# Hybrid decoder trunk on one core: ScalarE's table load at the top, the first chunk of x transposed as a whole, its rounding in pinned turns by K tile, the squares later

## The chip, the cores and the metric

The kernel runs on one core of one Trainium2 chip. The metric is device time in microseconds (us) of one execution, as the median of several. A core has five engines that run side by side, each in the order of its own instruction queue, and wait for each other by semaphores: TensorE (PE in the profile, its weight loads PEld), VectorE (DVE), ScalarE (ACT), GpSimd (POOL) and SyncE (SP, which here only issues transfers).

## The reference

The model has two layers over 256 tokens of width 2048. Each layer multiplies the normalised input by one wide projection, runs differential attention and a short gated convolution on the pieces, projects back, and then does a squared-ReLU MLP:

```python
for l in range(DEPTH):
    h = _rmsnorm(x, attn_norm_g[l])
    proj = h @ w_in[l]
    q, k, v, gate_b, gate_c, conv_in = jnp.split(proj, splits, axis=-1)
    ...
    x = x + jnp.concatenate([attn, conv.astype(attn.dtype)], axis=-1) @ w_out[l]
    hm = _rmsnorm(x, mlp_norm_g[l]) @ w_up[l]
    x = x + jnp.square(jax.nn.relu(hm)) @ w_down[l]
```

What matters for this case is the very first product, the first 512 columns of q in layer 0: `h @ w_in` over K = 2048. Nothing after it differs between the two kernels in work or order.

## The kernel before, in words

**Precision by halves.** Every fp32 matrix product is made of three products of a rounded type (fp32r). Each operand x is split into hi, which is x rounded by a ScalarE copy, and lo = x - hi, made by VectorE. The product is hi·hi + hi·lo + lo·hi (`TERMS`, L39). So each 128x512 block of weights costs one ScalarE instruction (`whi`, L291) and one VectorE instruction (`wlo`, L292) before TensorE can use it, and each block of activations costs a ScalarE `nT` (L255) and a VectorE `nT` (L256).

**The first product.** `linear` (L348 to L365) runs over 16 K tiles of 128 rows; I call them k0 to k15. A K tile takes six matmuls of 128x512: for each of the two token tiles hi·hi, then activation hi with weight lo, then activation lo with weight hi. The activations come from x by chunk: x is held in four chunks of 512 columns, and chunk n gives the K tiles 4n to 4n+3. The weights come in pieces, each of which holds two K tiles: piece p has the K tiles 2p and 2p+1 (`raw`, then `whi` and `wlo`). There are four buffers for `raw` and three each for `whi` and `wlo` (`wpool`, L111), so the rounding of piece p+3 has to wait until TensorE has used piece p up.

**A chunk.** `Norm.chunk` (L417 to L440) transposes a chunk on TensorE: eight 128x128 transposes into two PSUM banks (L425), two K tiles to a bank. Then `split_gained` (L253) rounds them: ScalarE `nT` hi with the norm's gain, VectorE `nT` lo. At the end two ScalarE squares with a running sum (`junk`, L437) collect the row sums that the norm needs; they are used only after all four chunks. The second instruction of ScalarE on a bank waits until VectorE has finished its first one on that bank.

**What sets the order.** TensorE's queue is in the order of the program. Pieces of work are put into it by a background list: `work.tick()` is called after each K tile (L364), and a piece that yields n is taken up again n ticks later. For the other engines a list scheduler picks the order from its own estimate of times; an instruction wrapped in `late` (L119) keeps its place in the program's order. `first_loads` (L1066) starts the chunks 1 to 3 with a delay of 4n-2 ticks, starts chunk 0 at once, ticks once, and then adds five warm-up matmuls of `ones` (L147). Chunk 0 transposes its first two K tiles, yields (L434), and transposes the other two after k0. With these delays the transposes of chunk n stand one K tile ahead of the first use: after k2, k6 and k10.

**The first transfers.** SyncE issues, in this order, the first half of chunk 0 of x, the first K tile of piece 0, the second half of chunk 0, the second K tile of piece 0, piece 1, chunk 1, pieces 2 and 3, chunks 2 and 3, and then piece 4 as soon as piece 0 is rounded. `by_dist`, `lamv` and the like are small setup for the attention, issued by GpSimd; `rps`, `vps` and `lps` are small matmuls of that setup, `rbc` (L470) is a matmul that spreads the norm's row factors, and `diag` is its input.

## Time and profile before

| | us |
|---|---|
| median of three runs | 2176.13 (2175.25 to 2177.49) |
| the profiled execution's own time | 2177.49 |
| span of its instructions in the profile | 2175.4 |
| TensorE busy | 2141.5 (98%) |
| VectorE busy | 1685.5 (77%) |
| ScalarE busy | 1291.3 (59%) |
| first matmul of q starts at | 7.49 |
| first matmul of k, the next product, starts at | 39.93 |

All times inside the profile count from the start of the span. A row of the timeline gives the start, the duration, the engine, the line, the operation, what is written and from what, the number of instructions that the row joins, and in brackets how long the engine was idle before it and which engine's instruction ended that idle time.

### The profile page before, as it was taken

The numbers are of one execution on the slowest core, as the hardware profiler recorded it, in microseconds if no ns is written. First come the engines' busy times: TensorE is split into PE (matmuls) and PEld (weight loads), VectorE is DVE, ScalarE is ACT, GpSimd is POOL, SyncE is SP. The second block draws the span as 40 slices with busy tenths as digits, with TensorE's granted clock in tenths as the row PEclk, the third lists the DMA queues.
The fourth block names the chain that finished last, engine by engine and source line by source line (L and its number), as shares of the span: only waits on it lengthen the run. The fifth ranks groups of instructions, "written<-read, shape, count | busy, mean of one in ns | idle before, by whom it ended". The sixth has DMA issues, their size and how long they took to land.

```text
span 2175.4 us, 29104 instructions
## 1 busy us (share of the span) xinstructions
PE 2141.5 (98%) x10978; PEld 1818.3 (84%) x10978; DVE 1685.5 (77%) x2341; ACT 1291.3 (59%) x1748; POOL 195.2 (9%) x264
## 2 busy tenths in 40 slices
PE   8999999999999999999999999999999999999999
PEld 7878888888888888788878788888888888887887
DVE  5677655698888888888756676556988888888886
ACT  6456545566666666555554564455666666665553
POOL 3021200000000000200101212000000000002001
PEclk9999999999999999999999999999999999999999
DMA  7654766477777777887655457655777777778884
GB/s 254 184 154 155 240 187 184 162 249 225 234 222 222 227 225 219 260 287 261 245 158 179 147 165 240 186 184 180 237 234 223 223 225 225 229 215 274 290 285 140
DMA packets 286012, 469.70 MB, mean 216 GB/s; under 512 B 10579, under 2 KB 191397, under 8 KB 283056
## 3 DMA queue, kind: packets, MB, share of 16 engines
q1 hardware_dynamic: 267552, 412.13, 60.7%
q0 software_dynamic: 18272, 55.70, 7.4%
q8 instruction: 86, 1.41, 0.3%
q14 instruction: 54, 0.44, 0.1%
q10 hardware_dynamic: 48, 0.02, 0.0%
HBM read 437.37 MB, written 30.43 MB: 215 GB/s over the span
## 4 chain that ended last, share of the span: by engine, by line
PE 92%; DVE 2%; DMA 2%; issue 2%; ACT 1%; POOL 1%; ACTq 0%; POOLq 0%; DVEq 0%
PE upc L855 29%; PE pr L903 12%; PE rt L1057 11%; PE o L361 8%; PE rt L903 4%; PE ci L383 4%; PE gc L383 4%; PE gb L383 4%; PE v L361 4%; PE k L361 4%; PE q L361 3%; DMA uraw<-in_w_up_dram 1%; PE upw L855 1%; PE sc L526 1%; PE pr L985 1%
## 5 line engine op out<-in xcount | busy, mean ns | idle before, releaser
L292 DVE TENSOR_TENSOR wlo<-raw,whi 128x1024 fp32r<-128x1024 f32 (+1 forms) x346 | 425.1, 1230 | 250.7 <-ACT whi L291 249.6
L291 ACT ACTIVATE whi<-raw 128x1024 fp32r<-128x1024 f32 (+1 forms) x346 | 363.9, 1054 | 420.7 <-PE o L361 73.6
L855 PE MATMUL upc<-nT,uhi 128*128 128x512 f32 x1920 | 477.6, 391 | 0.0
L718 ACT ACTIVATE uhi<-uraw 128x1024 fp32r<-128x1024 f32 x256 | 271.1, 1060 | 289.7 <-PE upc L855 254.1
L855 PEld LDWEIGHTS upc<-nT,uhi 128*128 128x128 f32 x1920 | 352.8, 188 | 68.2
L719 DVE TENSOR_TENSOR ulo<-uraw,uhi 128x1024 fp32r<-128x1024 f32 x256 | 312.3, 1220 | 115.4 <-ACT uhi L718 113.0
L855 PEld LDWEIGHTS upc<-nT,ulo 128*128 128x128 f32 x1920 | 261.9, 190 | 18.7
L855 PE MATMUL upc<-nT,ulo 128*128 128x256 f32 x1920 | 267.7, 282 | 0.0
L1057 PE MATMUL rt<-whi,g 128*128 128x512 f32 x672 | 211.1, 389 | 0.0
L361 PE MATMUL o<-whi,cat 128*128 128x512 f32 x512 | 159.5, 390 | 0.0
L1057 PEld LDWEIGHTS rt<-whi,g 128*128 128x128 f32 x672 | 126.1, 188 | 26.2
L1057 PE MATMUL rt<-wlo,g 128*128 128x512 f32 x336 | 130.7, 389 | 0.0
L361 PEld LDWEIGHTS o<-whi,cat 128*128 128x128 f32 x512 | 96.1, 188 | 19.7
L882 POOL DMA_DIRECT2D plain<-f x44 | 31.5, 716 | 830.8 <-DVE f L895 808.2
L895 DVE TENSOR_TENSOR f<-h,f 128x1024 fp32r<-128x1024 f32 (+1 forms) x84 | 102.1, 1216 | 0.0
L361 PE MATMUL o<-wlo,cat 128*128 128x512 f32 x256 | 99.7, 389 | 0.0
L740 DVE TENSOR_TENSOR t13l<-t,t13h 128x1024 fp32r<-128x1024 f32 x80 | 97.8, 1223 | 1.8 <-ACT t13h L739 0.5
L740 DVE TENSOR_TENSOR t24l<-t,t24h 128x1024 fp32r<-128x1024 f32 x80 | 97.3, 1216 | 0.4 <-ACT t24h L739 0.3
L903 PE MATMUL pr<-t13h,f 128*128 128x512 f32 x240 | 93.8, 391 | 0.0
L361 PE MATMUL q<-whi,nT 128*128 128x512 f32 x256 | 85.3, 404 | 3.4 <-ACT whi L291 3.4
L894 ACT ACTIVATE f<-h 128x1024 fp32r<-128x1024 f32 (+1 forms) x84 | 86.1, 1024 | 4.2 <-DVE h L892 4.1
L739 ACT ACTIVATE t24h<-t 128x1024 fp32r<-128x1024 f32 x80 | 84.0, 1050 | 4.5 <-PE rt L903 3.0
(365 smaller groups left out, 3879.1 us busy)
## 6 DMA issues: line engine op xcount, KB each, us to landing
uraw<-in_w_up_dram SPq DMA_DIRECT2D x128, 1024.0 KB, 6.5
raw<-in_w_in_dram SPq DMA_DIRECT2D x191, 512.0 KB, 4.0
draw<-in_w_down_dram SPq DMA_DIRECT2D x64, 1024.0 KB, 5.2
raw<-in_w_down_dram SPq DMA_DIRECT2D x64, 1024.0 KB, 6.2
raw<-in_w_out_dram SPq DMA_DIRECT2D x64, 512.0 KB, 3.7
plain<-f POOLq DMA_DIRECT2D x44, 512.0 KB, 6.4
g<-plain POOLq DMA_DIRECT2D x22, 1024.0 KB, 6.4
hid<-h POOLq DMA_DIRECT2D x20, 256.0 KB, 5.9
```

The costliest lines, as they stand in the source:

```text
L291: a = nc.scalar.activation(hi[:, k], raw[:, k], AF.Copy)
L292: d = nc.vector.tensor_sub(lo[:, k], raw[:, k], hi[:, k].bitcast(F32))
L361: nc.tensor.matmul(acc[:, t], a.ap[:, pa, k % KG, t * P:(t + 1) * P], (hi, lo)[pw][:, j], start=(k == 0 and n == 0), stop=(k == nk - 1 and ...
L383: nc.tensor.matmul(acc[:, f, 0] if part else acc[:, f], wt[:, k % 4, fs], a.ap[:, 0, k % KG] if part else a.ap[:, :, k % KG], start=(part ...
L718: nc.scalar.activation(hi, src, AF.Copy)
L719: nc.vector.tensor_sub(lo, src, hi.bitcast(F32))
L740: keep(nc.vector.tensor_sub(lo, src, hi.bitcast(F32)))
L855: nc.tensor.matmul(acc[:, 0] if part else acc, wt[:, k], a.ap[:, 0, k % KG] if part else a.ap[:, :, k % KG], start=(part == 0 and kh == 0 ...
L894: nc.scalar.activation(f[:, 0, :n], h[:, :n], AF.Copy)
L895: nc.vector.tensor_sub(f[:, 1, :n], h[:, :n], f[:, 0, :n].bitcast(F32))
L903: nc.tensor.matmul(prods[n], f[:, pa, a], b[pw], start=(start and m == 0), stop=(stop and m == 2))
L1057: nc.tensor.matmul(prods[p], blocks[b][:, slot, pa, 2 * k + t], w[pw][:, n], start=(i == PLAIN[0] and k == 0 and m == 0), stop=False)
```

## The change

The change touches only what is done before and during the first product.

1. A ScalarE copy of one column of `ones` into `ngains` is put at the top, so that ScalarE's table load, which precedes the first activation, no longer waits for `ngains`.
2. `Norm.begin` replaces `chunk(0, 0)`: all eight transposes of chunk 0 come before the first matmul of q. The five warm-up matmuls behind them and one tick are gone.
3. The activations of chunk 0 and the pieces 0 and 1 are rounded in turns by K tile (`in_turns`): for each of k0 to k3 ScalarE does `nT`, then `whi` of that K tile, and VectorE the two lo parts likewise. All of these are pinned by `late`. Pieces up to the eighth are pinned too when they are rounded (`halves`).
4. The squares of a chunk come later: six ticks after chunk 0's start, four ticks after the other chunks. `factors` waits for all of them.

```diff
+    ngains = const.tile([P, NG], F32, tag="ngains", name="ngains")
+    nc.scalar.activation(ngains[:, :1], ones[:, :1], AF.Copy)
     warm = bank("warm")
...
         def halves(self, raw, c=slice(None)):
-            first = self.cut and i < 2
-            for k in (slice(0, 1), slice(1, None)) if first else (slice(None),):
-                a = nc.scalar.activation(hi[:, k], raw[:, k], AF.Copy)
-                d = nc.vector.tensor_sub(lo[:, k], raw[:, k], hi[:, k].bitcast(F32))
-                if first:
-                    late(a)
-                    late(d)
-            return hi, lo
+            hi, lo = self.pair(raw)
+            a = nc.scalar.activation(hi, raw, AF.Copy)
+            d = nc.vector.tensor_sub(lo, raw, hi.bitcast(F32))
+            if self.cut and self.traced <= 8:
+                late(a)
+                late(d)
+            return hi, lo
...
+        def in_turns(self, n, split):
+            while self.traced < n:
+                self.traced += 1
+                raw = self.early.pop(0)
+                hi, lo = self.made[len(self.made)] = self.pair(raw)
+                for k in range(2):
+                    split(2 * self.traced - 2 + k)
+                    late(nc.scalar.activation(hi[:, k], raw[:, k], AF.Copy))
+                    late(nc.vector.tensor_sub(lo[:, k], raw[:, k], hi[:, k].bitcast(F32)))
...
                 self.tiles[n].ready = 2 * j + 2
-                if j == 0 and n == 0 and (self.which, self.l) == (0, 0):
-                    yield 1
+            if (self.which, self.l) == (0, 0):
+                yield 4
+            self.squares(n)
...
+        def begin(self, weights):
+            a = self.tiles[0].open()
+            tps = []
+            for j in range(2):
+                tps.append(bank(f"tpb{j}"))
+                for i in range(2):
+                    k = 2 * j + i
+                    for t in range(NT):
+                        nc.tensor.transpose(
+                            tps[j][:, i * S + t * P:i * S + (t + 1) * P],
+                            xs[0][:, t, k * P:(k + 1) * P], ident)
+            weights.in_turns(2, lambda k: split_gained(
+                a, k, tps[k // 2][:, k % 2 * S:(k % 2 + 1) * S], norm_gain(0, 0, k), late))
+            self.tiles[0].ready = KG
+            yield 6
+            self.squares(0)
...
-        work.start(norm.chunk(0, 0))
-        work.tick()
-        warm_up(5)
+        work.start(norm.begin(weights))
```

The order of the instructions moves on ScalarE, VectorE, GpSimd and TensorE up to about the middle of the next product, k, and is the same from there to the end; SyncE's order of transfers is the same throughout. Line numbers of the changed kernel differ: L255 becomes L256, L291 becomes L308 (in turns) or L287, L425 becomes L469 (chunk 0) or L439, L437 becomes L455, L361 becomes L374.

The first place is ScalarE at the start of q. Before, behind the table load (`nT_0` is chunk 0, `nT_1` chunk 1, `tpn` and `tpb` are the PSUM banks with the transposes; `whi` of 128x512 is one K tile of piece 0 or 1, of 128x1024 a whole piece):

```order
L255 ACTIVATE nT_0_162<-tpn_0_163,ngains 128x256 x2
L291 ACTIVATE whi<-raw 128x512 x2
L255 ACTIVATE nT_0_162<-tpn_1_191,ngains 128x256 x2
L437 ACTIVATE junk_0_200,ss_131<-x_83 128x512
L437 ACTIVATE junk_1_202,ss_131<-x_83 128x512
L291 ACTIVATE whi<-raw 128x512 x2
L291 ACTIVATE whi<-raw 128x1024 x2
L255 ACTIVATE nT_1_222<-tpn_0_223,ngains 128x256
```

In the changed kernel the same stretch, from the second K tile on, reads:

```order
L256 ACTIVATE nT_0_163<-tpb_164,ngains 128x256
L308 ACTIVATE whi<-raw 128x512
L256 ACTIVATE nT_0_163<-tpb_169,ngains 128x256
L308 ACTIVATE whi<-raw 128x512
L256 ACTIVATE nT_0_163<-tpb_169,ngains 128x256
L308 ACTIVATE whi<-raw 128x512
L256 ACTIVATE nT_1_220<-tpn_0_221,ngains 128x256
L256 ACTIVATE nT_1_220<-tpn_1_230,ngains 128x256
L256 ACTIVATE nT_1_220<-tpn_0_221,ngains 128x256
L256 ACTIVATE nT_1_220<-tpn_1_230,ngains 128x256
L287 ACTIVATE whi<-raw 128x1024 x2
L455 ACTIVATE junk_0_259,ss_132<-x_83 128x512
```

The two squares of chunk 0 have moved behind the pieces 2 and 3, and these two pieces (the `whi` of 128x1024) have moved behind all four `nT` of chunk 1.

The second place is TensorE around the transposes of chunk 1. Before (`q` is the sum in PSUM, `nT_0` and `nT_1` say which chunk a matmul uses):

```order
L425 MATMUL tpn_0_223<-ident,x_84 128x128 x4
L425 MATMUL tpn_1_232<-ident,x_84 128x128 x4
L361 MATMUL q_178<-whi,nT_0_162 128x512
L361 MATMUL q_178<-wlo,nT_0_162 128x512
L361 MATMUL q_178<-whi,nT_0_162 128x512 x2
L361 MATMUL q_178<-wlo,nT_0_162 128x512
L361 MATMUL q_178<-whi,nT_0_162 128x512
L361 MATMUL q_178<-whi,nT_1_222 128x512
```

In the changed kernel, from the last matmuls of k3 on:

```order
L374 MATMUL q_195<-wlo,nT_0_163 128x512
L374 MATMUL q_195<-whi,nT_0_163 128x512
L439 MATMUL tpn_0_221<-ident,x_84 128x128 x4
L439 MATMUL tpn_1_230<-ident,x_84 128x128 x4
L374 MATMUL q_195<-whi,nT_1_220 128x512
L374 MATMUL q_195<-wlo,nT_1_220 128x512
L374 MATMUL q_195<-whi,nT_1_220 128x512 x2
```

The six matmuls of k3 stood between the transposes of chunk 1 and the first matmul that uses them; now nothing stands there. The same holds for the chunks 2 and 3, whose transposes now stand directly ahead of k8 and k12.

The third place is ScalarE ahead of chunk 3. Before, with the semaphores that a row waits for:

```order
L291 ACTIVATE whi<-raw 128x1024 x2
L255 ACTIVATE nT_3_355<-tpn_0_356,ngains 128x256
L255 ACTIVATE nT_3_355<-tpn_1_365,ngains 128x256
L255 ACTIVATE nT_3_355<-tpn_0_356,ngains 128x256
L255 ACTIVATE nT_3_355<-tpn_1_365,ngains 128x256
L437 ACTIVATE junk_0_374,ss_131<-x_86 128x512
L437 ACTIVATE junk_1_376,ss_131<-x_86 128x512
L291 ACTIVATE whi<-raw 128x1024 x3
```

In the changed kernel the three `whi` are the pieces 6, 7 and 8, and the waits on PE are those for a free `whi` buffer:

```order
L287 ACTIVATE whi<-raw 128x1024 [waits DMAHW5_49,Activation_49]
L287 ACTIVATE whi<-raw 128x1024 [waits DMAHW6_49,PE_49,Activation_49]
L287 ACTIVATE whi<-raw 128x1024 [waits DMAHW7_49,PE_49,Activation_49]
L455 ACTIVATE junk_0_353,ss_132<-x_85 128x512 [waits DMAHW1_49]
L455 ACTIVATE junk_1_355,ss_132<-x_85 128x512
L256 ACTIVATE nT_3_357<-tpn_0_358,ngains 128x256 [waits PE_49]
L256 ACTIVATE nT_3_357<-tpn_1_367,ngains 128x256 [waits PE_49]
L256 ACTIVATE nT_3_357<-tpn_0_358,ngains 128x256 [waits DVE_49]
L256 ACTIVATE nT_3_357<-tpn_1_367,ngains 128x256 [waits DVE_49]
```

Piece 8, which only the next product uses and whose buffer is free once k11 is done, now stands ahead of chunk 3, and so do the squares of chunk 2.

More of the change, by code (lines that the diff above doesn't have):

```diff
@@ L161, in trunk @@
     nc.tensor.transpose(gps[:, :NG], ngv, ident[:NG, :NG])
-    ngains = const.tile([P, NG], F32, tag="ngains", name="ngains")
     nc.vector.tensor_copy(ngains, gps[:, :NG])
@@ L283, in halves, with pair @@
         def halves(self, raw, c=slice(None)):
-            i = len(self.made)
-            shape = [P] + list(raw.shape[1:])
-            hi = wpool.tile(shape, F32R, tag="hi", name="whi")
-            lo = wpool.tile(shape, F32R, tag="lo", name="wlo")
-            first = self.cut and i < 2
-            for k in (slice(0, 1), slice(1, None)) if first else (slice(None),):
-                a = nc.scalar.activation(hi[:, k], raw[:, k], AF.Copy)
-                d = nc.vector.tensor_sub(lo[:, k], raw[:, k], hi[:, k].bitcast(F32))
-                if first:
-                    late(a)
-                    late(d)
-            return hi, lo
+            hi, lo = self.pair(raw)
[5 more added lines that the diff above has]
+            return hi, lo
+        def pair(self, raw):
+            shape = [P] + list(raw.shape[1:])
+            return (wpool.tile(shape, F32R, tag="hi", name="whi"),
+                    wpool.tile(shape, F32R, tag="lo", name="wlo"))
+        def in_turns(self, n, split):
[7 more added lines that the diff above has]
+                    late(nc.vector.tensor_sub(lo[:, k], raw[:, k], hi[:, k].bitcast(F32)))
         cut = False
@@ L432, in chunk, with squares @@
                 self.tiles[n].ready = 2 * j + 2
-                if j == 0 and n == 0 and (self.which, self.l) == (0, 0):
-                    yield 1
+            if (self.which, self.l) == (0, 0):
+                yield 4
+            self.squares(n)
+        def squares(self, n):
+            self.squared += 1
             for t in range(NT):
@@ L440, in chunk @@
                     late(sq)
+        def begin(self, weights):
[14 more added lines that the diff above has]
+            self.squares(0)
         def factors(self):
-            while not all(t.ready == KG for t in self.tiles):
+            while self.squared < D // CH or not all(t.ready == KG for t in self.tiles):
                 yield 1
```

9 lines of the change are left out of this document (5 added, 4 removed).

## The prediction

> **What bounds the kernel now.** I read the page first, for the engine that decides, then the windows of the first 50 us.
>
> ```profile
> PE   2141.5 (98%) x10978; PEld 1818.3 (84%) x10978; DVE 1685.5 (77%) x2341; ACT 1291.3 (59%) x1748; POOL 195.2 (9%) x264
> PE 92%; DVE 2%; DMA 2%; issue 2%; ACT 1%; POOL 1%; ACTq 0%; POOLq 0%; DVEq 0%
> ...
> 0.00:10.00 10.00, 7.09 (x36) 5.91 (x37) 2.71 (x8) 3.27 (x5) 6.79 (x18) 1.00 0.76 244
> 10.00:20.00 10.00, 7.84 (x31) 6.00 (x31) 7.19 (x15) 7.45 (x17) 0.62 (x2) 0.83 0.99 339
> 20.00:30.00 10.00, 10.00 (x47) 7.60 (x46) 6.11 (x10) 7.81 (x16) 0.00 (x0) 1.00 0.49 164
> 30.00:40.00 10.00, 9.57 (x48) 7.58 (x46) 6.37 (x16) 5.78 (x11) 4.03 (x5) 1.00 0.80 225
> ...
> 40.28 15.01 PE k L361 x66
> ```
>
> TensorE is busy for 98% of the span and carries 92% of the chain. So an edit counts only by how much earlier or later it lets TensorE reach the next product, k; from there the order is as before. The windows (length, then busy time of PE, PEld, DVE, ACT and POOL, granted clock, DMA share, GB/s) show idle TensorE and a lowered clock only in the first 20 us, apart from 0.43 us before 40. The chain's row gives the price of a matmul: 15.01 us for 66, 0.227 each, 1.36 a K tile.
>
> ```profile
> 1.72 0.43 SPq L135 DMA_DIRECT2D x<-in_x_dram  x1
> 2.19 0.47 SPq L314 DMA_DIRECT2D raw<-in_w_in_dram  x1
> 2.69 0.43 SPq L316 DMA_DIRECT2D raw<-in_w_in_dram  x1
> x<-in_x_dram SPq DMA_DIRECT2D x1, 256.0 KB, 4.8
> raw<-in_w_in_dram SPq DMA_DIRECT2D x1, 256.0 KB, 5.1
> raw<-in_w_in_dram SPq DMA_DIRECT2D x1, 512.0 KB, 6.2
> 4.01 0.92 PE L425 MATMUL tpn<-ident,x 128*128 128x128 f32 x4 [0.20 <-DMA x<-in_x_dram]
> 4.13 1.28 ACT L255 ACT_TABLE_LOAD   x1 [4.13 <-DVE ngains L163]
> 5.42 0.47 ACT L255 ACTIVATE nT<-tpn,ngains 128x256 fp32r<-128x256 f32 x1
> 7.49 0.50 PE L361 MATMUL q<-whi,nT 128*128 128x512 f32 x1 [1.45 <-ACT whi L291]
> 11.54 0.62 ACT L437 ACTIVATE junk<-x 128x512 f32<-128x512 f32 x1
> 12.77 3.03 ACT L291 ACTIVATE whi<-raw 128x512 fp32r<-128x512 f32 x4
> 13.44 0.50 PE L361 MATMUL q<-whi,nT 128*128 128x512 f32 x1 [1.93 <-ACT whi L291]
> 15.50 0.63 PE L361 MATMUL q<-whi,nT 128*128 128x512 f32 x1
> 15.93 1.91 PE L425 MATMUL tpn<-ident,x 128*128 128x128 f32 x8
> 17.48 0.78 PE L361 MATMUL q<-whi,nT 128*128 128x512 f32 x1
> 18.85 0.39 PE L361 MATMUL q<-wlo,nT 128*128 128x512 f32 x1
> ```
>
> The start has two waits on ScalarE: q begins at 7.49 after 1.45 us, and k2 at 13.44 after 1.93 us, because the squares from 11.54 stand ahead of piece 1. From 14.83 to 18.24 the clock is half: matmuls 0.43 us apart (15.50 to 15.93), transposes 1.91 us for eight. k3 starts at 17.48 with one matmul left at half clock and ends at about 19.2.
>
> **The change part by part.** *Table load.* It now needs only `ones`, so its 1.28 us lies under the wait for x, and `nT` of k0 starts when its transposes end, 4.01 + 0.92 + 0.04 = 4.97 instead of 5.42. The added copy of one column is an operation that the trace lacks; 256 columns take the `nT` 0.47, so one column takes between 0 and 0.47. I take nothing, since it ends before 3 us and `ngains`, which now waits for it, waits for its transposed gains anyway; without that cover it would cost up to 0.47, and a gain below nothing is excluded, since it adds work.
>
> *Whole chunk first.* The second half of chunk 0 lands at 1.72 + 4.8 = 6.5; four more transposes at 0.11 put the first matmul of q at 6.96, which is 0.5 earlier. The five warm-up matmuls filled idle time only.
>
> *Turns and squares.* The weights of k1 land at 2.19 + 5.1 = 7.3; their `whi` (half a piece's 1.05, 0.6) and `wlo` (0.7) let its second matmul run at 8.7, some 0.2 late; a matmul's successor after a wait is 0.1 late as well. Piece 1 lands at 2.69 + 6.2 = 8.9, and by the same two steps k2's second matmul runs at 10.3, again 0.3 in all. k3 finds its parts made. So four K tiles from 6.96 take 4 × 1.36 + 0.6 and end at 13.0. Eight transposes later it is 13.9. Before, that state was reached at 19.2. TensorE is 5.3 us ahead. SyncE's queue has the same order; piece 4 is issued when piece 0 is rounded, as before, and piece 5 some 3 us sooner, well ahead of use.
>
> ```profile
> 23.38 1.03 PE L425 MATMUL tpn<-ident,x 128*128 128x128 f32 x8
> 24.02 1.94 ACT L255 ACTIVATE nT<-tpn,ngains 128x256 fp32r<-128x256 f32 x4 [0.69 <-PE tpn L425]
> 24.53 1.95 DVE L256 SCALAR_TENSOR_TENSOR nT<-tpn,ngains,nT 128x256 fp32r<-128x256 f32 x4
> 25.86 0.62 ACT L437 ACTIVATE junk<-x 128x512 f32<-128x512 f32 x1
> 27.08 1.05 ACT L291 ACTIVATE whi<-raw 128x1024 fp32r<-128x1024 f32 x1
> 28.16 1.22 DVE L292 TENSOR_TENSOR wlo<-raw,whi 128x1024 fp32r<-128x1024 f32 x1 [1.69 <-ACT whi L291]
> 16.03 0.41 DVE L221 TENSOR_TENSOR lprod<-lamv 1x256 f32<-1x256 f32 x1
> 17.50 0.40 DVE L223 TENSOR_REDUCE ldots<-lprod 1x4 f32<-1x256 f32 x1
> 39.61 0.67 PE L470 MATMUL rbc<-diag,ones 128*128 128x256 f32 x2 [0.43 <-DVE s_gain L217]
> ```
>
> *k4: most of the lead is paid back.* The transposes of chunk 1 now stand right before k4, and ScalarE does four `nT` before piece 2. From 13.0: 0.64 to the first `nT` (24.02 - 23.38), 1.94 for four, 1.05 for `whi`: 16.6, when the first matmul of k4 may run. VectorE does its four `nT`, then `lprod` and `ldots` (0.8), until 16.6, then `wlo`, 1.22: the second matmul runs at 17.87. Had k4 run through, it would have begun at 17.6; before it began at 19.2. The lead is 1.6.
>
> *Half clock again.* Whether the clock falls is read from stretches of the length of the slow ones, on their grid:
>
> ```profile
> 4.59:8.00 3.41, 1.96 (x14) 1.45 (x12) 1.50 (x3) 2.80 (x5) 2.75 (x6) 1.00 0.95 278
> 11.42:14.83 3.41, 1.25 (x5) 0.77 (x5) 1.78 (x3) 3.41 (x9) 0.00 (x0) 1.00 1.05 375
> 14.83:18.24 3.41, 3.41 (x14) 2.92 (x13) 3.35 (x6) 1.75 (x5) 0.00 (x0) 0.50 0.97 333
> 124.06:127.47 3.41, 1.84 (x9) 1.18 (x7) 1.86 (x4) 2.13 (x6) 1.93 (x5) 1.00 0.69 172
> 127.47:130.89 3.42, 2.71 (x19) 2.43 (x19) 2.46 (x4) 1.56 (x6) 0.11 (x1) 1.00 0.54 158
> 1096.86:1100.27 3.41, 1.25 (x8) 1.15 (x9) 3.08 (x8) 2.25 (x6) 0.36 (x1) 1.00 0.77 240
> 1100.27:1103.68 3.41, 3.41 (x10) 2.64 (x9) 1.05 (x3) 0.47 (x1) 0.00 (x0) 0.50 0.34 127
> ```
>
> Two stretches with PE busy for 1.25 us are followed by 3.41 us at half clock; one with 1.84 is followed by full clock. On the same grid the changed kernel's stretch 14.83 to 18.24 holds under 1 us of matmuls, so 18.24 to 21.66 runs at half and costs 3.41 × (1 - 0.227/0.43) = 1.6. The slow stretch of before is in the 19.2. The lead is 0.
>
> *k8.* The transposes of chunk 2 lose their cover of one K tile: k8 starts 0.64 + 0.47 + 0.06 = 1.17 after they begin, not 0.9. Cost 0.3.
>
> *k12.* ScalarE's queue now has the rounding of piece 8, then two squares, ahead of the `nT` of chunk 3, and piece 8 waits for the buffer that k11 frees. From the end of k11: 1.05 + 2 × 0.61 + 0.47 and latencies, less overlaps, is 2.8; the transposes take 0.9 of it. Cost 1.9 to 2.0. Queued behind that wait are piece 9 and the bias copies, which nobody needs yet.
>
> *rbc.* Before, TensorE waited 0.43 for VectorE's small work, `diag` among it, in front of `rbc`. Now `rbc` stands after five K tiles of k and `diag` is ready: gain 0.4.
>
> *A second slow stretch.* The stretch around k12 has 2.0 us without matmuls, so PE is busy for about 1.4 us if all of it falls into one stretch: nearer to the 1.25 that was followed by half clock than to 1.84. I take 1.6; its ends are 0 and 1.6.
>
> **Sum**, against the profiled execution: -1.6 at k4, +1.6 for the clock, +0.3, +2.0, -0.4, together +1.9; small extra waits where lo parts come late in k8 and k12 (0.3, between 0 and 0.5, the wait for a `wlo` at k4's second matmul being the longest such row); +1.6 for the second stretch: **+3.8**. That makes 2181.3 beside its own 2177.49 (span 2175.4). The median is 1.36 below that execution. By the median it is 2179.9; since a stretch need not lie on the same grid in each execution, I take 2179.8, +0.17%.
>
> **The rivals.** *A, the lead holds.* If k4 and k12 did not wait, the 5.3 of lead, 0.5 of it from the start, would stay, less 0.3, plus 0.4: 2176.1 - 5.4 = 2170.7. For it speaks that ScalarE has free time (busy for 7.45 of the 10 us to 20); against it that the changed queue puts the four `nT` of chunk 1 ahead of piece 2, and that they cannot begin before k3 ends.
>
> *B, break-even: the clock stays full.* The waits come as worked out, but neither is long enough to lower the clock: 1.9 + 0.3 - 1.6 = +0.6, 2176.7. Before, a gap of 1.93 us in 11.42 to 14.83 was enough, and the gaps at k4 are 2.7 and 1.1, so the rows speak against it; it would take a different grid. The Trainium skill has a rule by which this rival wins: "TensorE: Matmul & The Clock Gate", section "Why this matters for your kernels", asks only for no idle gap over about 3 us between bursts of matmuls. By that rule the sum would be +0.6 and by the rows it is +3.8; the trace disagrees with the rule, since half clock followed a gap of 1.93 us.
>
> *C, slower by over 0.2%: the first stretch falls too.* The five warm-ups lay in 4.59 to 8.00, whose PE busy of 1.96 held half its time from them. Now that stretch has 1.0 us of q and about 0.5 of transposes, 1.5, between 1.25 and 1.84. If the border is over 1.5, then k0 to k3 run at half clock from 8.00 to 11.42. Some of it hides behind the waits for piece 1, the rest, about 1.1, shifts everything: 2179.9 + 1.1 = 2181.0.
>
> **How the numbers follow.** Within 0.2% means 2171.8 to 2180.5, about what a measurement of this kernel can tell from no change. My forecast (waits at k4 and k12, one or two slow stretches, 2178 to 2181) has 0.70, of which a quarter lies over 2180.5; A 0.04, B 0.12, C 0.14. Faster 0.04, same 0.64, slower 0.32. The range leaves out A and the outer tails: the low end is B's 2176.7, the high end C with the upper end of the lo waits and some spread of the median, 2181.9.
>
> **What would show it.** In the changed kernel's profile: q begins near 7.0; k3 ends near 13.0; TensorE then waits for ScalarE's `whi` of piece 2 and VectorE's `wlo` and goes on at 17.9; the clock is 0.50 for one stretch soon after; before k12 there are 2 us of idle time behind ScalarE's `nT`; `rbc` has no wait; k begins 3 to 4 us later than 39.93. I am wrong if k4 starts by 15, if the clock stays at 1.00 after 18, or if anything past the first 60 us changes by more than the slow stretches, which also appear at 1100, come and go.

## The result and the profile after

| | before | after |
|---|---|---|
| median, us (lowest to highest) | 2176.13 (2173.31 to 2178.97) | 2181.14 (2177.92 to 2188.37) |
| runs | 22 | 22 |
| ratio to before, 95% interval | | 1.0026 (1.0019 to 1.0032) |
| profiled execution, own time | 2177.49 | 2179.62 |
| its span | 2175.4 | 2177.7 |
| first matmul of q, k4, k8, k12, k, v starts | 7.49, 19.30, 25.64, 32.96, 39.93, 62.89 | 7.13, 17.92, 28.21, 37.77, 45.55, 68.72 |

The changed kernel is slower by 5.0 us by the medians, and the interval lies wholly above 1: a small loss, of a quarter of a per cent. The last row of the table tells where it arises. At k4 the changed kernel is still ahead, at k8 it is 2.6 us behind, at k12 4.8, at k 5.6, and at v 5.8. In this one profiled execution the span is only 2.3 longer, so 3.5 us come back behind v. Matching the same matmuls in both traces shows where: 1.7 at 1100, where before has a stretch at half clock and this execution has none; 1.2 between 1495 and 1565, where TensorE waits 0.9 less for `ev` and `f` of the MLP; and a net 0.6 ahead of 470, again without half clock. Such differences come and go between executions; the medians, over 22 runs each, lie 5.0 apart, close to the 5.6 at k.

TensorE's timeline of the changed kernel, with lines left out at `...` (start, duration, engine, line, operation, count; in brackets the idle time and who ended it):

```profile
6.39 1.09 PE L469 MATMUL tpb<-ident,x 128*128 128x128 f32 x4 [1.26 <-DMA x<-in_x_dram]
7.13 0.78 PE L374 MATMUL q<-whi,nT 128*128 128x512 f32 x1
10.69 0.63 PE L374 MATMUL q<-whi,nT 128*128 128x512 f32 x2
...
14.35 1.04 PE L439 MATMUL tpn<-ident,x 128*128 128x128 f32 x8
17.92 0.79 PE L374 MATMUL q<-whi,nT 128*128 128x512 f32 x1 [2.54 <-ACT whi L287]
19.39 0.79 PE L374 MATMUL q<-wlo,nT 128*128 128x512 f32 x1 [0.68 <-DVE wlo L288]
...
27.05 1.03 PE L439 MATMUL tpn<-ident,x 128*128 128x128 f32 x8
28.21 0.50 PE L374 MATMUL q<-whi,nT 128*128 128x512 f32 x1
...
34.83 1.03 PE L439 MATMUL tpn<-ident,x 128*128 128x128 f32 x8
37.77 0.62 PE L374 MATMUL q<-whi,nT 128*128 128x512 f32 x1 [1.91 <-ACT nT L256]
...
45.55 0.39 PE L374 MATMUL k<-whi,nT 128*128 128x512 f32 x1
```

Read the durations before the waits. The first matmul of q takes 0.78 us and two matmuls after 10.69 take 0.63 together: up to 10.69 TensorE ran at half speed. It did so again behind the wait at 17.92 (0.79) and, from 38.00 on, behind that at 37.77 (0.62, part of it at full speed). The brackets give the three waits: 2.54 and 0.68 us at k4, 1.91 at k12. At k8 there is no bracket; its start is 1.16 behind that of the transposes.

The clock changes only on a grid of stretches of 3.41 us. The windows of the changed kernel, cut along that grid (length; busy us of PE, PEld, DVE, ACT, POOL; granted clock; DMA share; GB/s), put a number on this:

```profile
3.86:7.28 3.42, 2.00 (x9) 1.64 (x10) 1.76 (x4) 1.47 (x3) 3.02 (x7) 1.00 0.94 265
7.28:10.69 3.41, 3.41 (x9) 2.65 (x9) 2.06 (x5) 2.50 (x5) 1.03 (x2) 1.00 1.05 377
...
14.10:17.52 3.42, 1.29 (x10) 0.94 (x8) 1.92 (x5) 2.42 (x5) 0.00 (x0) 1.00 1.01 362
17.52:20.93 3.41, 2.33 (x5) 1.54 (x6) 2.91 (x4) 3.41 (x8) 0.00 (x0) 0.50 0.20 41
20.93:24.34 3.41, 3.41 (x10) 2.63 (x9) 1.48 (x4) 0.15 (x2) 0.00 (x0) 0.50 0.95 321
...
34.58:38.00 3.42, 1.51 (x11) 1.16 (x10) 1.48 (x2) 2.93 (x7) 1.81 (x2) 1.00 0.70 200
38.00:41.41 3.41, 3.41 (x9) 2.58 (x9) 1.50 (x4) 0.94 (x3) 0.02 (x1) 0.50 0.85 243
...
130.16:133.57 3.41, 1.50 (x7) 0.92 (x5) 1.71 (x4) 1.82 (x6) 2.05 (x5) 1.00 0.74 187
133.57:136.98 3.41, 3.00 (x20) 2.68 (x20) 2.27 (x4) 1.59 (x7) 0.20 (x1) 1.00 0.52 166
```

The stretch with the wait at k4 holds 1.29 us of PE work, and the next one runs at 0.50. That next one holds 2.33, but at half speed, which is 2.33 × 0.227/0.43 = 1.2 at full speed, and so the one after it is at 0.50 as well. The stretch with the wait at k12 holds 1.51, and is followed by 0.50; the last two rows, for comparison, are 1.50 followed by 1.00. The column says 1.00 for the first two rows, although nine matmuls fill 3.41 us there (0.38 each, against 0.227): the clock's record begins only with the rise at 10.69, so ahead of it one has to go by the durations.

ScalarE's timeline of the changed kernel shows both waits from the other side:

```profile
14.99 1.94 ACT L256 ACTIVATE nT<-tpn,ngains 128x256 fp32r<-128x256 f32 x4 [4.42 <-PE tpn L439]
16.82 1.99 ACT L287 ACTIVATE whi<-raw 128x1024 fp32r<-128x1024 f32 x2
...
35.07 1.06 ACT L287 ACTIVATE whi<-raw 128x1024 fp32r<-128x1024 f32 x1 [2.63 <-PE q L374]
36.04 0.61 ACT L455 ACTIVATE junk<-x 128x512 f32<-128x512 f32 x1
...
37.26 0.81 ACT L256 ACTIVATE nT<-tpn,ngains 128x256 fp32r<-128x256 f32 x2
```

ScalarE stood idle for 4.42 us until the transposes of chunk 1, and only then did the four `nT` and, behind them, piece 2. At k12 the row at 35.07 is piece 8, which waited 2.63 for its buffer; two squares follow (the second is left out here), and the `nT` of chunk 3, for which TensorE stood, come last. VectorE adds its part at k4:

```profile
17.80 0.41 DVE L224 TENSOR_REDUCE ldots<-lprod 1x4 f32<-1x256 f32 x1
18.13 2.34 DVE L288 TENSOR_TENSOR wlo<-raw,whi 128x1024 fp32r<-128x1024 f32 x2
```

The low parts of piece 2 start at 18.13, behind two small setup operations (`ldots` is the second), and TensorE goes on at 19.39.

### The profile page after: what moved, and what is told of

Its sections match the earlier page's. It is cut to its first block, busy times and chain, and to the rows that moved or that the text cites. A ratio compares the mean times of both kernels' runs of the same rounds, so it can differ in the third digit from the quotient of the medians.

```text
span 2177.7 us, 29085 instructions
## 1 busy us (share of the span) xinstructions
PE 2142.8 (98%) x10968; PEld 1819.7 (84%) x10968; DVE 1687.5 (77%) x2341; ACT 1291.3 (59%) x1749; POOL 196.0 (9%) x264
## 4 chain that ended last, share of the span: by engine, by line
PE 95%; DVE 2%; ACT 1%; DMA 1%; issue 1%; POOL 0%; SPq 0%; DVEq 0%; ACTq 0%
PE upc L891 30%; PE pr L939 13%; PE rt L1093 10%; PE o L374 8%; PE rt L939 4%; PE q L374 4%; PE gc L396 4%; PE ci L396 4%; PE gb L396 4%; PE v L374 4%; PE k L374 4%; PE upw L891 1%; PE sc L562 1%; PE pr L1021 1%; PE av L601 0%
## 5 line engine op out<-in xcount | busy, mean ns | idle before, releaser
L288 DVE TENSOR_TENSOR wlo<-raw,whi 128x1024 fp32r<-128x1024 f32 x342 | 422.8, 1238 | 247.9 <-ACT whi L287 246.5
L287 ACT ACTIVATE whi<-raw 128x1024 fp32r<-128x1024 f32 x342 | 361.2, 1059 | 426.7 <-PE o L374 73.6
L374 PE MATMUL o<-whi,cat 128*128 128x512 f32 x512 | 159.5, 390 | 0.0
L374 PEld LDWEIGHTS o<-whi,cat 128*128 128x128 f32 x512 | 96.1, 188 | 19.8
L374 PE MATMUL o<-wlo,cat 128*128 128x512 f32 x256 | 99.6, 389 | 0.0
L374 PE MATMUL q<-whi,nT 128*128 128x512 f32 x256 | 87.1, 413 | 4.6 <-ACT whi L287 2.5
```

The costliest lines, as they stand in the source:

```text
L287: a = nc.scalar.activation(hi, raw, AF.Copy)
L288: d = nc.vector.tensor_sub(lo, raw, hi.bitcast(F32))
L374: nc.tensor.matmul(acc[:, t], a.ap[:, pa, k % KG, t * P:(t + 1) * P], (hi, lo)[pw][:, j], start=(k == 0 and n == 0), stop=(k == nk - 1 and ...
```

## The experiments

My theory after the result: each of the two waits leaves too little TensorE work in a stretch of 3.41 us, and the half clock that follows costs as much as the wait. The waits have one root, that the transposes of a chunk stand directly ahead of their first use. In the expectations this is Q: the waits at k4 and k12, which ScalarE's queue ends, with the half clock behind them as one of its terms. The rivals: the five missing warm-ups are the cause, which leave the clock low at the start (C, as in the prediction); or the waits themselves are, and the clock only goes along with them; or the squares or the table load cost what the kernel loses. Where an expectation starts from the changed kernel's 2181.1, that stood beside 2176.13 for the kernel before; beside the runs that kernel had 2177.06 to 2177.67, so compare the differences. The eleven runs, each with the median of the kernel before on the same chip:

| run | median (range) | before | ratio (95%) | full clock first at | half clock later, under 140 us | k starts | v starts |
|---|---|---|---|---|---|---|---|
| e1_warm | 2181.27 (2177.64 to 2186.58) | 2177.67 | 1.0020 (1.0011 to 1.0029) | 9.96 | 20.20, 37.26 | 44.81 | 67.99 |
| e2_tick | 2174.71 (2172.61 to 2177.79) | 2177.67 | 0.9987 (0.9978 to 0.9996) | 9.32 | none | 36.51 | 61.13 |
| e3_early | 2180.04 (2174.95 to 2182.28) | 2177.67 | 1.0011 (1.0002 to 1.0020) | 10.12 | 34.01, 129.58 | 41.30 | 64.48 |
| e4_fill | 2178.01 (2174.39 to 2181.92) | 2177.67 | 1.0003 (0.9994 to 1.0011) | 4.99 | none | 40.06 | 63.24 |
| e5_squares | 2176.47 (2174.61 to 2179.45) | 2177.29 | 0.9997 (0.9988 to 1.0006) | 6.14 | 129.02 | 38.11 | 62.15 |
| e6_table | 2176.78 (2173.49 to 2178.67) | 2177.29 | 0.9994 (0.9985 to 1.0003) | 8.03 | 14.86 | 39.81 | 62.76 |
| e7_no_warm | 2180.35 (2177.59 to 2183.09) | 2177.29 | 1.0011 (1.0002 to 1.0020) | 11.14 | 130.61 | 41.10 | 64.06 |
| e8_tick_early | 2175.59 (2172.10 to 2178.63) | 2177.29 | 0.9992 (0.9983 to 1.0001) | 9.61 | none | 35.44 | 61.26 |
| e9_tick_early_bias | 2174.73 (2171.06 to 2178.26) | 2177.06 | 0.9989 (0.9980 to 0.9998) | 4.95 | 124.41 | 35.40 | 58.58 |
| e10_tick_bias | 2174.53 (2171.65 to 2179.12) | 2177.06 | 0.9991 (0.9982 to 1.0000) | 10.30 | 126.35 | 37.01 | 60.19 |
| e11_squares2 | 2180.27 (2177.15 to 2184.15) | 2177.06 | 1.0016 (1.0007 to 1.0025) | 11.76 | 18.58 (twice 3.41) | 44.37 | 67.55 |

For comparison, the profiled execution of before has full clock first at 4.59 and half clock at 14.83, that of after 10.69, and 17.52 (twice 3.41) and 38.00. The columns on the clock and on k and v are of the one profiled execution of each kernel; the medians are of all its runs.

**The warm-ups put back into the changed kernel** (between the two banks of transposes of chunk 0).

```diff
                             xs[0][:, t, k * P:(k + 1) * P], ident)
+                if j == 0:
+                    warm_up(5)
             weights.in_turns
```

> The changed kernel with the five warm-up matmuls put back, between the two banks of transposes of chunk 0. Theory Q (the loss lies in ScalarE's queue ahead of k4 and k12) expects only the start to mend: the clock is full well before 10.7 us, k3 ends some 1.3 us earlier than 14.35, and the waits ahead of k4 and k12 stay as long; about 2180, 1 us below the changed kernel's 2181.1. Theory C (the loss is the clock, which the missing warm-ups leave low at the start) expects most of the 5 us back: 2177 or less.

Measured: +3.6 by the medians, against +5.0 without the warm-ups; the intervals overlap, and C's 2177 or less did not come. The waits are those of the changed kernel (2.54 and 0.77 at k4, 1.91 at k12). The clock rose at 9.96 in this execution, so here the warm-ups did not bring full clock to the start of q. Where the warm-ups stand, and so the start of q, differs from the kernel before; the next run settles that they are not the main cause, since it leaves them out.

**The tick put back** (the transposes of chunk n stand one K tile ahead of their use again).

```diff
         work.start(norm.begin(weights))
+        work.tick()
```

> The changed kernel with the one background tick put back behind the start of chunk 0, so that the transposes of the chunks 1, 2 and 3 stand one K tile earlier on TensorE, and ScalarE's nT of chunk 3 stand ahead of piece 8 and the squares. Theory Q expects k12 to lose its wait of 1.9 us and k8 its 0.3, and k4's wait to shrink by the 1.36 of a K tile, 3.6 in all, and one slow stretch less: 2176 to 2177.5. Theory C expects under 1 us, since the warm-ups are still gone: above 2180.

Measured: 3.0 us under the kernel before, 0.9987 (0.9978 to 0.9996). One line turns the loss into a small gain, larger than Q had expected and with the warm-ups still left out. TensorE's timeline of this run at chunk 1:

```profile
12.05 1.03 PE L439 MATMUL tpn<-ident,x 128*128 128x128 f32 x8
...
15.63 0.49 PE L374 MATMUL q<-whi,nT 128*128 128x512 f32 x1 [1.14 <-ACT whi L287]
16.89 0.50 PE L374 MATMUL q<-wlo,nT 128*128 128x512 f32 x1 [0.77 <-DVE wlo L288]
```

The transposes come before k3, whose matmuls lie under ScalarE's `nT`. The wait for piece 2 falls from 2.54 to 1.14, its matmuls take 0.49 rather than 0.79, and no stretch at half clock follows. At k12 nothing is waited for. The waits fell by about what was expected, but all three stretches at half clock of the changed kernel went, where I had counted one. k starts 3.4 us before that of the kernel before, though the clock rose only at 9.32.

**The pieces rounded earlier** (the roundings may run 2i instead of i - 1 pieces ahead at piece i; no tick).

```diff
-            ahead = min(max(i - 1, 0), AHEAD) if self.cut else AHEAD
+            ahead = min(2 * i, AHEAD) if self.cut else AHEAD
```

> The changed kernel with the pieces 2 and 3 rounded ahead of the nT of chunk 1 on ScalarE (the look-ahead of the weights is longer at k2), TensorE's order untouched. Theory Q expects k4 to begin about 1.2 us after k3's end instead of 3.6, with no second wait for its lo part, some 3.5 us gained; but piece 6, whose buffer k7 frees, and two squares now stand ahead of the nT of chunk 2, a new wait of about 2 us at k8. Net 1.5 to 3 us gained with the clock, 2178 to 2179.6. Theory C expects no change over 1 us.

Measured: +2.4, 1.0011. The wait at k4 is gone, and k4 starts at 15.00 with no half clock behind it. But now k8 waits 1.91 as well (23.84, for `nT`), k12 still does (33.43), and the half clock of 34.01 follows that. So removing the wait at k4 mends about half of the 5.0, as Q had it, and the wait moves to the next chunk as long as the transposes stand directly ahead of their use.

**The idle time filled with unused matmuls** (ten of `ones` behind the transposes of the chunks 1 and 3; the kernel does work that nobody reads).

```diff
                 self.tiles[n].ready = 2 * j + 2
+            if (self.which, self.l) == (0, 0) and n != 2:
+                extra = bank(f"fill{n}")
+                for _ in range(10):
+                    nc.tensor.matmul(extra[:, :P], ones, ones, start=True, stop=True)
```

> The changed kernel with ten unused matmuls of ones (128x128) behind the transposes of the chunks 1 and 3, so that TensorE is busy for about 2.2 us of each of the two waits, which themselves stay. It prices the slow stretches behind the waits. Theory Q with its clock term expects the stretches at half clock behind k4 and k12 to go, 1.6 us for each of them, 3 to 4.8 us: 2176.5 to 2178. If the clock were not lowered by the waits, nothing would change: 2181.

Measured: +0.3, 1.0003 (0.9994 to 1.0011). Its timeline of TensorE:

```profile
12.71 1.03 PE L439 MATMUL tpn<-ident,x 128*128 128x128 f32 x8
13.58 2.40 PE L450 MATMUL fill<-ones 128*128 128x128 f32 x20
16.28 0.50 PE L374 MATMUL q<-whi,nT 128*128 128x512 f32 x1 [0.30 <-ACT whi L287]
17.74 0.50 PE L374 MATMUL q<-wlo,nT 128*128 128x512 f32 x1 [0.96 <-DVE wlo L288]
...
31.73 2.40 PE L450 MATMUL fill<-ones 128*128 128x128 f32 x20
```

Nothing useful came earlier: k4's first matmul stands 3.6 us behind its transposes, as in the changed kernel (17.92 - 14.35), and k12's follows 2.15 us of filling. Only the clock stayed full up to k, and k starts at 40.06, 5.5 us before that of the changed kernel and within 0.2 of before. This is the cleanest split of the loss. The waits as such only use up the lead, and the half clock is the loss. The record of every execution, not of the profiled ones alone, says the same: it has the mean granted clock, which is 0.9948 over the 22 executions of the changed kernel and 0.9970 over the 11 of this run. The difference, 0.0022 of 2178 us, is 4.8 us of clock. Of the 5.5, up to 1.6 (transposes of chunk 1 at 12.71 instead of 14.35) is due to the start, where the two kernels do not differ and this execution happened to reach full clock at 4.99; the medians, which hold many starts, give 4.7 us between the two (+0.3 against +5.0).

**The squares later, in the kernel before** (six and four ticks; the norm's factors wait for all of them).

```diff
                     yield 1
+            if (self.which, self.l) == (0, 0):
+                yield 6 if n == 0 else 4
+            self.squared += 1
             for t in range(NT):
                 junk = wide(f"junk{n}_{t}")
...
-            while not all(t.ready == KG for t in self.tiles):
+            while self.squared < D // CH or not all(t.ready == KG for t in self.tiles):
```

> The kernel before with part 4 of the change alone: the squares of a chunk six or four ticks later, nothing else. Theory Q (ScalarE's queue ahead of a use) expects the two squares to leave the place ahead of piece 1, k2 to start some 1.2 us sooner than 13.44, the stretch 11.42 to 14.83 to hold over 1.84 us of matmuls so that no half clock follows (1.6 us), and the wait ahead of rbc to go (0.4): k starts 3 us earlier than 39.93. Some of it may be given back where the row factors come later, as in the run with the tick (1.2 us at a transpose of q). 1.5 to 3 us below before. Theory C (the warm-ups and the clock's start) expects the clock's start as before and no more than the 1.2 us.

Measured: -0.8, no difference that can be told (0.9988 to 1.0006), where I had expected 1.5 to 3. The trace shows the gain and its loss. k2 waits 0.71 rather than 1.93, the half clock at 14.83 is gone, and k starts 1.8 earlier; but v starts only 0.7 earlier. The lead is lost inside k, which the runs e8 to e10 take up.

**The table load first, in the kernel before** (the copy of one column of `ones` at the top, with `ngains` set up there, nothing else).

> The kernel before with part 1 alone: the table load at the top. Both theories expect the first nT near 5.0 instead of 5.42, the first matmul of q near 7.05 instead of 7.49, and 0.4 us at most in the end, which the times cannot tell from nothing.

```diff
+    ngains = const.tile([P, NG], F32, tag="ngains", name="ngains")
+    nc.scalar.activation(ngains[:, :1], ones[:, :1], AF.Copy)
     warm = bank("warm")
...
-    ngains = const.tile([P, NG], F32, tag="ngains", name="ngains")
     nc.vector.tensor_copy(ngains, gps[:, :NG])
```

Measured: -0.5, 0.9994 (0.9985 to 1.0003), k 0.1 earlier; the wait of 1.93 at k2 and its half clock stand as before. q begins at 7.36, not at the 7.05 expected, in an execution whose clock is full only from 8.03. By itself the table load is worth nothing that these times can tell.

**The five warm-ups left out of the kernel before.**

```diff
         work.tick()
-        warm_up(5)
```

> The kernel before without the five warm-up matmuls behind the first transposes. Theory C expects the clock to reach full speed one or two stretches later and the kernel to lose most of the changed kernel's 5 us. Theory Q expects a loss of 0 to 1.5 us, as far as half clock at k0 and k1 is not hidden by the wait at k2, and none of the waits of the changed kernel.

Measured: +3.1 by the medians, 1.0011 (1.0002 to 1.0020) by the ratio, more than Q's 1.5 and less than C's most of 5. The window of this run behind the first transposes:

```profile
4.31:7.73 3.42, 1.07 (x4) 0.67 (x4) 0.99 (x3) 2.73 (x5) 3.04 (x7) 1.00 0.99 313
```

Without the warm-ups 4.31 to 7.73 holds 1.07 us of PE work, and full clock comes at 11.14. k starts 1.2 us later than in before's profile. The stretch at half clock at 130.61, which that one lacks, adds 1.6, but it follows a gap that both kernels have (shown below, with the bias copies). So the warm-ups of the kernel before are worth something, 1.2 us in this trace, and that part of rival C holds; how the rest of the 3.1 comes about is not shown. Full clock came at 4.59, 6.14 and 8.03 in the three profiles with the start of before, and between 9.32 and 11.76 in six of the eight that start as the changed kernel does (4.95 and 4.99 in the other two).

**Tick and earlier rounding together.**

```diff
-            ahead = min(max(i - 1, 0), AHEAD) if self.cut else AHEAD
+            ahead = min(2 * i, AHEAD) if self.cut else AHEAD
...
         work.start(norm.begin(weights))
+        work.tick()
```

> The changed kernel with the tick put back and the pieces 2 and 3 rounded ahead of the nT of chunk 1, both. Theory Q expects the waits at k4 (1.14 and 0.77 us in the run with the tick alone) to go as well, and no new wait at k8, since three of the four nT of chunk 2 stand ahead of piece 6: 1.5 to 2 us below the run with the tick, some 4.5 us below before. Theory C expects no difference to the run with the tick.

Measured: -1.7, a miss: I had expected it to go well under the run with the tick alone. All waits at k4, k8 and k12 are down to one of 0.56, and k starts 4.5 us before that of before. But v starts only 1.6 before. ScalarE's timeline in k:

```profile
43.26 0.64 ACT L249 ACTIVATE bias<-rev 128x512 f32<-128x512 f32 x1 [3.32 <-DMA rev<-by_dist_d]
43.80 0.67 ACT L523 ACTIVATE q00sq<-q,rowf 128x512 f32<-128x512 f32 x1
44.37 1.05 ACT L287 ACTIVATE whi<-raw 128x1024 fp32r<-128x1024 f32 x1
```

and TensorE's timeline of the same run, some 10 us on:

```profile
50.71 0.50 PE L374 MATMUL k<-wlo,nT 128*128 128x512 f32 x1 [0.82 <-DVE wlo L288]
...
55.26 0.66 PE L540 MATMUL q00tp<-ident,q00n 128*128 128x128 f32 x4 [1.28 <-DVE q00n L531]
```

The second copy of the position bias waits 3.32 us for the transfer of `rev`. It is needed only by the attention, which first reads `bias` at 89.8 here, but the square for q's normalisation and the rounding of the next weights are queued behind it, and TensorE then waits 0.82 and 1.28. The transfer lands at about 43.3 here and at 45.1 in the kernel before, where the copy waits 0.41 for it. So whoever reaches k much earlier meets a copy whose data are still on the way.

**The copies of the bias 4 ticks later**, with tick and earlier rounding, and with the tick alone.

```diff
             revs.append(rev)
-        yield 4
+        yield 8 if l == 0 else 4
```

> The changed kernel with the extra tick and the earlier rounding of the run before, and besides the copies of the position bias (ScalarE, bias from rev) put 4 ticks later in the program. Theory R: k started 4.5 us ahead of the kernel before in the run without the later copies, and v only 1.6 ahead, because ScalarE stood 3.3 us at a bias copy until the transfer of rev landed at 43.3, and the roundings and squares queued behind it came late; TensorE then waited 0.8 for a low part and 1.3 for the normalised q. With the copies behind those roundings both waits go, v starts some 2.5 us earlier than in the run before (near 58.7), and the median comes to 2172.5 to 2173.5. Rival S: the chain of q's normalisation (square, reduction, GpSimd, scaling) sets k's end whatever ScalarE does with the bias: q00n is waited for again, v stays at 61, and the median at 2175 to 2176.

> The changed kernel with the extra tick alone, and the copies of the position bias 4 ticks later. Theory R: k at 36.5 as with the tick alone, the wait of 1.2 us for the normalised q goes, v starts near 59.5 rather than 61.1, and the median comes to 2173 to 2174. Rival S: v stays at 61, the median at 2174.5 to 2175.

In the first of the two, ScalarE's timeline now reads:

```profile
39.46 0.69 ACT L523 ACTIVATE q00sq<-q,rowf 128x512 f32<-128x512 f32 x1
42.44 1.06 ACT L287 ACTIVATE whi<-raw 128x1024 fp32r<-128x1024 f32 x1 [2.28 <-DMA raw<-in_w_in_dram]
```

The square of q runs at 39.46 instead of 43.80, TensorE has no wait in k, and v starts at 58.58, 2.7 us before that of the run without this edit (61.26) and 4.3 before that of before. With the tick alone v starts at 60.19 instead of 61.13, although k starts 0.5 later; from k to v both kernels take 23.18 us, against 25.82 and 24.62 without the edit. Theory R is shown for the place, and rival S falls: v did not stay at 61. The medians did not follow it all the way. They are 2174.73 (expected 2172.5 to 2173.5) and 2174.53 (2173 to 2174), 2.3 and 2.5 under before. In both profiled executions a stretch at half clock at 124 to 130 takes 1.6 us back, which e8 and e2, the same kernels without the edit, do not show. The edit does not make the gap behind which it comes. It is the same in the kernel before and in e9:

```profile
128.18 0.41 PE L587 MATMUL atp<-ident,ao 128*128 128x128 f32 x2 [2.29 <-DVE ao L583]
```

```profile
123.89 0.41 PE L623 MATMUL atp<-ident,ao 128*128 128x128 f32 x2 [2.30 <-DVE ao L619]
```

All thirteen profiled executions have it, 2.29 to 2.32 us long, and half clock follows in five of them (e3, e5, e7, e9, e10). What differs is where the borders of the stretches cut it, as in e8 and in e9:

```profile
122.24:125.65 3.41, 2.04 (x9) 1.34 (x8) 2.06 (x4) 2.33 (x6) 1.81 (x4) 1.00 0.64 171
```

```profile
121.00:124.41 3.41, 1.11 (x8) 0.72 (x7) 1.71 (x3) 1.13 (x2) 1.96 (x5) 1.00 0.71 241
```

Why the medians gained less than v did stays open. The four kernels with the tick are equal within their intervals; three of them (e2, e9, e10) have the lowest ratios here, 0.1% under before.

**Chunk 2's squares at their old place**, in the changed kernel.

```diff
-            if (self.which, self.l) == (0, 0):
+            if (self.which, self.l) == (0, 0) and n != 2:
                 yield 4
             self.squares(n)
```

> The changed kernel, but with chunk 2's two squares right behind its activations again, as in the kernel before; those of chunks 0 and 1 stay late. Theory Q: the squares that stand ahead of chunk 3's activations, 36.04 to 37.3, make 1.2 us of the 1.9 that TensorE waits at k12; the wait falls to 0.7, and with more TensorE work in that stretch the second stretch at half clock goes as well: k starts 1.2 to 2.8 us earlier than 45.6 (for the same clock ahead of it), and the median falls by 1 to 3 us, to 2178 to 2180. Rival T: piece 8's rounding alone, which waits for the buffer of K tile 11, sets the end of the wait: 1.9 us stay, the second stretch at half clock too, and the median stays within 1 us of 2181.

TensorE's timeline of this run at k12, behind the transposes at 35.60:

```profile
37.33 0.50 PE L374 MATMUL q<-whi,nT 128*128 128x512 f32 x1 [0.69 <-ACT nT L256]
38.62 0.72 PE L374 MATMUL q<-whi,nT 128*128 128x512 f32 x2 [0.56 <-DVE nT L257]
```

and its window there:

```profile
35.64:39.06 3.42, 2.17 (x13) 1.46 (x12) 2.03 (x4) 2.25 (x5) 1.83 (x2) 1.00 0.86 256
```

The wait is 0.69 instead of 1.91, as theory Q had it, and rival T falls. The stretch holds 2.17 us of PE work, and full clock follows. The second term that Q named, the half clock behind k12, is gone; the wait at k4 and the two stretches at half clock behind it stand as they were. The median is 3.2 over before instead of 5.0; the upper end of Q's range was missed by 0.3 (as a difference to before it would be +3.9, and +3.2 lies inside), and in this execution the clock rose a microsecond later (11.76) than in that of after, so k starts only 1.2 earlier.

## Why the prediction was right, and where its size was off

Forecast 2179.8, between 2176.7 and 2181.9; measured 2181.14. The mechanism is the one forecast: the lead of the start is paid back at k4, k12 waits, and half clock follows both. I had put the result 1.3 us too low, and with that inside 0.2% of before; it lies just outside (+0.23% by the medians, 0.26% by the ratio), where rival C's time stood (2181.0). The sum came out closer than its terms: two of them were too small by 1.5 and 0.9 us. Step by step:

- **Table load: 0.** Alone it moved k by 0.1 and the median by 0.5, which can't be told from nothing (e6).
- **q begins at 6.96.** Measured 7.13. The second half of x landed as worked out; from there the four transposes took 0.74 rather than 0.46, at half speed.
- **k3 ends at 13.0: this step failed.** It ended at 14.35. I had priced four K tiles at 1.36, full clock from the start, as the kernel before had it from 4.59. In the changed kernel the clock was half until 10.69. This is what rival C had, though not as C put it: the clock did not fall after a full start, it had not risen yet. In the kernels that start alike the same transposes stand at 12.71, 13.84 and 14.80 where full clock comes at 4.99, 10.12 and 11.76 (e4, e3, e11). So the price held for an early rise, and whether it held in a given execution was luck.
- **k4 goes on at 17.87.** Measured 19.39, 1.5 later: the 1.35 of k3, and 0.2 more in the chain. ScalarE's steps were as worked out: 0.64 to the first `nT` (14.99), four of them, piece 2. On VectorE the prediction added up short: by its own rows the four `nT`, `lprod` and `ldots` end 3.9 after the transposes begin (1.15 + 1.95 + 0.8), at 16.9 and not at 16.6; measured, `wlo` started 3.8 after.
- **One stretch at half clock behind k4, 1.6: the other step that was mis-sized.** There were two, 17.52 to 24.34. From the restart (19.39 less 0.27, had there been no wait inside k4) four K tiles at full speed would have ended at 24.57; they ended at 27.05. The half clock cost 2.5, not 1.6. I had read the border from stretches at full clock and did not ask what a stretch that is itself at half clock and holds a wait would count for. The two other kernels that keep k4's waits show half clock behind it as well, one stretch in e1 and two in e11.
- **k8: +0.3.** k8 started 1.16 behind its transposes; forecast 1.17.
- **k12: +2.0.** 1.91 in the row at 37.77, by the queue that was named; e11 shows 1.2 of it to be the two squares.
- **A second slow stretch, +1.6, at k12.** It came, 38.00 to 41.41, behind 1.51 us of PE work, with the wait whole inside one stretch; so it did in e1 (37.26) and e3 (34.01), which keep that wait. A border of the grid inside the wait would leave more work in both stretches.
- **rbc: -0.4.** It stands in k, at 52.35, without a wait; the new order reaches to the middle of k, past the first product.
- **Small waits for low parts, +0.3.** No bracket of that kind in k8 to k15.

The forecast for k was 3.8 later, the trace has 5.6: +1.5 at k4's restart and +0.9 for the second half stretch, and some 0.6 less for the rest. Three of the signs that were named beforehand came out otherwise: k began 5.6 us later instead of 3 to 4, the clock was 0.50 for two stretches instead of one, and past 60 us 1.8 of the 3.5 us that came back are small waits, not slow stretches. Against rival A, the lead did not hold. Against rival B, the clock did not stay full; e4 shows what B's time would have been, 0.3 over before, which is close to the +0.6 that B had. The Trainium skill ("TensorE: Matmul & The Clock Gate", section "Why this matters for your kernels") asks only for no idle gap over about 3 us. No gap here is that long (2.54 and 0.68 at k4, 1.91 at k12), the clock fell behind both waits, and filling the gaps kept it up, so the trace goes against that figure.

What stays open: how often full clock comes late in the kernel before and in the changed one over many executions, since only profiled executions show when the clock rose (the mean granted clock of a profiled execution counts from the rise on); and why the runs with the bias copies later gained less in the median than v gained in the trace.

## What to carry to other kernels

When a change moves a TensorE step that others read directly ahead of its first use, look for what stood between the two: here six matmuls covered the activations, and the one tick that puts them back there was worth some 8 us (from 5.0 over before to 3.0 under). Price a TensorE wait twice, once as the wait and once as the half clock behind it, and count the TensorE work per stretch rather than the length of the gap; where the borders of the stretches lie is chance, so the half clock is a price with a probability. A lead that is won early counts only up to the next queue whose order was laid out for the old times; here it was a copy that nobody needed for another 45 us, at the head of ScalarE's queue.

## What the runs showed of the hardware

**When the clock falls.** At full clock, stretches of 3.41 us with 1.25 to 1.29 us of PE work were followed by half clock, and so was one with 1.51; with 1.84, 2.17 and 2.25 (at k4 in e2) they were not. Another one of the changed kernel held 1.50, in 130.16 to 133.57, and was followed by full clock. Cut along the grids of all thirteen traces, every full-clock stretch with 1.38 us or less was followed by half clock and every one with 1.58 or more by full clock; between them both occur (1.50 in e3 and 1.55 in e5 were followed by half; 1.55 in e1 and 1.57 in e3 by full). So the border is near 1.5, and the ends of matmuls in the profile are modelled, so that a hundredth is not to be trusted.

**When it rises at the start.** The first stretch at full clock came behind a stretch that was nearly filled, at half speed. In the kernel before, and in the run with the filling matmuls:

```profile
1.18:4.59 3.41, 3.21 (x14) 2.82 (x15) 0.19 (x1) 0.46 (x1) 3.21 (x7) 1.00 0.66 212
```

```profile
1.58:4.99 3.41, 3.35 (x15) 2.56 (x13) 0.19 (x1) 1.11 (x2) 3.31 (x8) 1.00 0.81 263
```

3.21 and 3.35 us, and full clock at once. In the run with the table load alone and in the one with the warm-ups put back:

```profile
1.21:4.62 3.41, 3.09 (x13) 2.70 (x14) 0.19 (x1) 1.48 (x2) 3.24 (x7) 1.00 0.69 223
```

```profile
3.13:6.55 3.42, 2.99 (x14) 2.59 (x14) 0.79 (x3) 1.11 (x3) 3.42 (x8) 1.00 0.90 267
```

3.09 and 2.99, and one more stretch at half speed. (The column shows 1.00 ahead of the first rise because the record of the clock begins there.) The grid of stretches lies differently in each execution, so the same start has full clock at 4.95 or at 11.76. While the clock was still half, a stretch that held the wait for the second half of x (0.8 to 1.3 us in after, e2, e3 and e8) was lost: 2.00 us of PE work in 3.86 to 7.28, for instance. The warm-ups of e1 filled that gap, but ran 2.34 us at half speed, so that q began at 8.01 instead of 7.13.

**Busy time at half clock counts for less.** 2.33 us of busy time at half clock did not bring the clock back (17.52 to 20.93 of the changed kernel), though 1.84 at full clock was enough to keep it. Later in the traces 2.71 at half clock was not enough either (e11, 919.70) and 2.90 was (e10, 1993.44). Times 0.227/0.43 these are 1.43 and 1.53 us of work at full speed, so an estimate puts both borders at about the same work. The start does not fit it: 3.09 there would be 1.63, and the clock did not rise. Why is open.
